# Attention queries regrouped by GpSimd copies, and end blocks padded with zeros to 128 rows, in an encoder layer on one core

## The chip, the cores and the metric

The kernel runs on one core of a Trainium2 chip. Time is device time in microseconds of one execution, and the median of several runs is the number that counts. The traces quoted here come from one further execution under the profiler.

## What is computed

One layer of a bidirectional encoder over 2048 tokens of width 1024: an input projection, eight heads of dilated attention, four heads of a gated recurrence (HGRN2), an output projection, and a mixture of 16 experts. The change touches the attention alone. Each head of width 64 runs three patterns, and in each of them the sequence falls into `dilation` interleaved subsequences, inside which a query sees the keys up to 64 places away:

```python
DILATED_PATTERNS = ((128, 1), (512, 4), (2048, 16))

def dilated_window_attention(q, k, v, window, dilation, slopes):
    half = window // (2 * dilation)          # 64 in every pattern
    ...
    band = jnp.abs(delta) <= half
    mask = band & key_ok
    bias = -slopes[:, None, None] * (dilation * jnp.abs(delta))
    s = jnp.einsum('brnqhd,brnkhd->brnhqk', qs, ks)
    s = jnp.where(mask, s + bias, NEG_INF)
    m = jnp.max(s, axis=-1, keepdims=True)
    e = jnp.exp(s - m)
    den = jnp.sum(e, axis=-1)
    num = jnp.einsum('brnhqk,brnkhd->brnqhd', e, vs)
```

The three numerators are then added with weights exp(m - max m) and divided by the denominators added in the same way.

## The kernel before

A scheduler orders the instructions of each engine ahead of time, by priorities: "mixer" work (recurrence, attention) goes first, and matmuls of the projections ("fill", into the PSUM tile `pm`) stand wherever the scheduler expected TensorE to be free. The order is fixed in the program, and each engine executes its own list in order.

The stages are: norm and input projection with the recurrence heads between its matmuls (0 to 850 us), then attention with the rest of the projection and half of the output projection as filler (850 to 1477 us), then the other half of the output projection, the routing and the experts.

In attention, `att_turn` transposes a quarter of the sequence (512 tokens, tile `x4`) into `qs` (queries) and `kh`, `kl` (keys, high and low part), with the 64 channels of a head on partitions and a second copy of them below for the low part of the queries. Both are stored in token order. `att_head` then goes through four quarters `g`. In each, `four(0, ..)` and `four(1, ..)` do four units of 128 queries for patterns 0 and 1 (dilation 1 and 4), and in the first quarter all 16 units of pattern 2 (dilation 16) are done as well. `block` takes two units (pattern 2: four):

- scores: per unit two matmuls into the PSUM tile `pS`. The stationary operand is `qs[:, q0:q0 + dil*127 + 1:dil]`, 128 queries with a step of `dil`; the moving operands are 256, 192 (at an end of a subsequence) or 128 keys of `kh` and `kl`, with the same step;
- VectorE adds the bias table and finds the extreme value (line 612), ScalarE takes exp (line 613), TensorE transposes the result in pieces (line 618), VectorE or ScalarE copies it to `eT` (lines 622 to 635), and TensorE multiplies it with the values `vp` into `pn` (line 641, two passes each). At an end of a subsequence one of the two pieces has 64 rows instead of 128.

The quarter's results go through DRAM (`num_d`), since patterns 0 and 2 hold the tokens in another arrangement: `n0` and `n2` are written by DMA, read back into `cb` beside pattern 1's result `cb[:, 2]`, combined on VectorE (lines 689 to 698), and written to `mix_d`. `cb` has three buffers that take turns over quarters.

Of the kernel before, what the change touches and what calls it, by code (L numbers as in the profile page):

```python
# [45 lines left out]
def encoder_layer(ctx, tc, x, norm1_w, w_in, q_norm_w, k_norm_w, lb_f, lb_b, o_norm_w, w_out,  # L46
# [454 lines left out]
    def att_setup(p):  # L501
        T = {}
        dl = p.tile([128, 512], F32, name="ex", bufs=4)
        T["ad"], T["mk"] = [], []
        for v, (base, w) in enumerate(((-64, 256), (0, 128))):
            a = p.tile([128, w], F32, name=f"ad{v}", bufs=1)
            pool.iota(dl[:, :w], pattern=[[1, w]], base=base, channel_multiplier=-1,
                      allow_small_or_imprecise_dtypes=True)
            dve.tensor_scalar(a, dl[:, :w], -1.0, None, op0=OP.mult)
            dve.tensor_tensor(a, a, dl[:, :w], op=OP.max)  # L510
            m = p.tile([128, w], F32, name=f"mk{v}", bufs=1)
            dve.tensor_scalar(m, a, 64.5, 1e30, op0=OP.is_gt, op1=OP.mult)
            T["ad"].append(a)
            T["mk"].append(m)
        wq = p.tile([128, 1], F32, name="wq", bufs=1)
        wk = p.tile([128, 1], F32, name="wk", bufs=1)
        for s in range(2):
            pool.dma_start(wq[s * 64:(s + 1) * 64, :], q_norm_w.rearrange("o d -> d o"))
            pool.dma_start(wk[s * 64:(s + 1) * 64, :], k_norm_w.rearrange("o d -> d o"))
        dve.tensor_scalar(wq, wq, -0.125, None, op0=OP.mult)  # L520
        T["wq"], T["wk"] = wq, wk
        for n in ("qs", "kh", "kl"):
            T[n] = p.tile([128, S], F32R, name=n, bufs=1)

        T["vp"] = [p.tile([128, n, 65], F32, name=f"vp{i}", bufs=1) for i, n in enumerate((17, 20, 16))]
        for vp in T["vp"]:
            dve.memset(vp[:, :, 64:65], 1.0)
        return T

    def att_load(p, T, h, g):  # L530

        u, s2 = h // 2, h % 2
        for j in range(2):

            x4 = p.tile([128, 4, 128], F32, name="x4", bufs=4)
            sp.dma_start(x4[:, :, :64],
                         dram_ap(qk_d, (u * S + g * 512) * 256 + 128 * j + 64 * s2,
                                 [[256, 128], [128 * 256, 4], [1, 64]]))
            pool.tensor_copy(x4[:, :, 64:], x4[:, :, :64])
            T["x4", g, j] = x4  # L540

    def att_values(T, h, g):

        voff = 64 * h
        v0, v1 = T["vp"][0], T["vp"][1].rearrange("p (r b) c -> p b r c", b=5)
        for b in (g, 4)[:1 + g // 3]:
            lo, n = (0, 64) if b == 0 else (128 * b - 64, 128 if b < 4 else 64)
            sp.dma_start(v1[:n, b, :, :64], dram_ap(v_d, voff + lo * 2048, [[2048, n], [512, 4], [1, 64]]))
        if g == 0:
            sp.dma_start(v0[:64, 0, :64], dram_ap(v_d, voff, [[512, 64], [1, 64]]))  # L550
        b0 = max(4 * g, 1)
        sp.dma_start(v0[:, b0:4 * g + 4, :64],
                     dram_ap(v_d, voff + (128 * b0 - 64) * 512, [[512, 128], [128 * 512, 4 * g + 4 - b0], [1, 64]]))
        if g == 3:
            sp.dma_start(v0[:64, 16, :64], dram_ap(v_d, voff + (S - 64) * 512, [[512, 64], [1, 64]]))

    def att_turn(T, g):

        sl = slice(g * 512, (g + 1) * 512)
        qs, kh, kl = T["qs"], T["kh"], T["kl"]  # L560
        for j in range(2):
            pt = (pa, pb)[j]()
            for i in range(4):
                pe.transpose(pt[:, i * 128:(i + 1) * 128], T["x4", g, j][:, i], ident)
            if j == 0:
                act.activation(qs[:, sl], pt, AF.Copy, scale=T["wq"])
                dve.scalar_tensor_tensor(qs[64:, sl], pt[64:], T["wq"][64:], qs[64:, sl].bitcast(F32),
                                         op0=OP.mult, op1=OP.subtract)
# [8 lines left out]
    def att_head(p, T, h):  # L577
# [2 lines left out]
        tabs = []  # L580
        for pat, (tw, v) in enumerate(((256, 0), (256, 0), (128, 1))):
            tab = p.tile([128, tw], F32, name=f"tab{pat}", bufs=2 - pat // 2)
            dve.scalar_tensor_tensor(tab, T["ad"][v], slope * 4 ** pat, T["mk"][v], op0=OP.mult, op1=OP.add)
            tabs.append(tab)

        def unit(pat, n):

            if pat == 2:
                return n, 16, n, 0, 128, [(0, 128, n)]
# [4 lines left out]
            blk = [(lo, 128 - lo, b0 + i), (128, hi - 128, b0 + i + 1)]  # L594
            return r + dil * 128 * i, dil, r + dil * (128 * i - 64 + lo), lo, hi, blk

        def block(pat, n0, units, w, nst, pnum):
# [5 lines left out]
            for j, (q0, dil, k0, lo, hi, blk) in enumerate(units):  # L603
# [5 lines left out]
            for j, (q0, dil, k0, lo, hi, blk) in enumerate(units):  # L609
# [4 lines left out]
            sizes = []  # L614
            for j, un in enumerate(units):
                for lo, nk, b in un[5]:
                    c = j * w + lo // 128 * 128
                    pe.transpose(pT[:nk, c:c + 128], ex[:, j * w + lo:j * w + lo + nk], ident)  # L618
                    sizes.append(nk)
            if min(sizes) == 128:  # L620
                if n0 % 8 < 6:
                    dve.tensor_copy(eT, pT)  # L622
                else:
                    act.activation(eT, pT, AF.Copy)
            elif sizes[:2] == sizes[2:]:
                for i in range(2):
                    ev, pv = (t[:sizes[i]].rearrange("p (j i c) -> p i j c", j=2, i=2)[:, i] for t in (eT, pT))
                    act.activation(ev, pv, AF.Copy)
            else:
                c = 0  # L630
                while c < 4:
                    e = c + 1
                    while e < 4 and sizes[e] == sizes[c]:
                        e += 1
                    act.activation(eT[:sizes[c], c * 128:e * 128], pT[:sizes[c], c * 128:e * 128], AF.Copy)
                    c = e
            for j, un in enumerate(units):
                nb = len(un[5])
                for i, (lo, nk, b) in enumerate(un[5]):
                    c = j * w + lo // 128 * 128  # L640
                    pe.matmul(pnum[:, n0 % 4 + j, :], eT[:nk, c:c + 128], vp[:nk, b, :],  # L641
                              start=i == 0, stop=i == nb - 1)

        def four(pat, n4, nst):

            per = 4 if pat == 2 else 2
            pnum = pn([128, 512])[:, :260].rearrange("p (j c) -> p j c", j=4)
            for n in range(n4, n4 + 4, per):
                block(pat, n, [unit(pat, n + i) for i in range(per)], 512 // per, nst, pnum)
            act.activation(nst[:, :, :65], pnum, AF.Copy)  # L650

        for g in range(4):
            cb = p.tile([128, 3, 4, 66], F32, name="cb", bufs=3)
            n0 = p.tile([128, 4, 66], F32, name="n0", bufs=2)
            four(0, 4 * g, n0)
            row = g * 512 * 66
            sp.dma_start(dram_ap(num_d, h * S * 66 + row, [[66, 128], [128 * 66, 4], [1, 66]]), n0)
# [175 lines left out]
    with mixer():  # L835
# [3 lines left out]
        for g in range(4):  # L839
            att_load(ap_, AT, 0, g)  # L840
            att_values(AT, 0, g)
            if g < 2:
                att_turn(AT, g)
    heads(0)
    unit_qk(2)
# [345 lines left out]
```

## Time and profile before

| | |
|---|---|
| median of 3 runs | 2837.08 us (2824.97 to 2841.68) |
| profiled execution | 2828.04 us, of which the trace spans 2825.4 us |
| attention stage in the trace | 850.3 to 1476.9 us |
| TensorE busy over the span | 2728.9 us (97%) |
| VectorE, ScalarE, GpSimd busy | 1775.3, 1453.8, 128.3 us |

The profiled execution has 2.6 us around its span. Busy time of TensorE counts overlapping matmuls, so what a matmul costs is read from the distance between the starts of neighbours, not from its duration.

### The profile page before, as it was taken

Reading aid. Unit: us, or ns where it says so; the run is one execution under the profiler, and the core shown is the slowest. Engines: PE = TensorE matmul, PEld = TensorE weight load, DVE = VectorE, ACT = ScalarE, POOL = GpSimd, SP = SyncE. Lnnn points to the kernel's source line nnn. Section 1 sums busy time; section 2 is a strip of 40 time slices with the busy share of each in tenths; the row PEclk is TensorE's granted clock in tenths of the full one; section 3 lists DMA queues with packets and bytes.
Section 4 is the critical chain, followed back from the end, with each engine's and each line's share of the span. In section 5 each row is a group of like instructions: output and inputs, shape, how many; then the busy total and the mean of one; then the engine's idle time right before and its main releaser. Section 6 shows DMA issues by size and latency. Waiting matters only on the chain.

```text
span 2825.4 us, 59470 instructions
## 1 busy us (share of the span) xinstructions
PE 2728.9 (97%) x23462; PEld 2574.3 (91%) x23462; DVE 1775.3 (63%) x4396; ACT 1453.8 (51%) x2829; POOL 128.3 (5%) x157
## 2 busy tenths in 40 slices
PE   8999999999999999999999959999999999999998
PEld 8999999899999999989898849999999999999997
DVE  6627887888865455756566565555555555555553
ACT  6636666677645444644354434444444444444442
POOL 0000000000000000000000000000000000000000
PEclk9999999999999999999999969999999999999999
DMA  9887767777767555555547526666666666666663
GB/s 301 258 248 215 235 210 226 208 228 231 222 209 201 153 133 157 152 161 157 146 131 274 175 73 212 206 206 208 209 209 209 208 208 207 207 207 206 206 196 102
DMA packets 557062, 558.73 MB, mean 198 GB/s; under 512 B 142944, under 2 KB 507488, under 8 KB 556784
## 3 DMA queue, kind: packets, MB, share of 16 engines
q1 hardware_dynamic: 547248, 521.31, 59.1%
q0 software_dynamic: 9536, 33.64, 5.3%
q8 instruction: 184, 3.01, 0.4%
q14 instruction: 94, 0.77, 0.1%
HBM read 453.92 MB, written 100.93 MB: 196 GB/s over the span
## 4 chain that ended last, share of the span: by engine, by line
PE 83%; DMA 8%; DVE 7%; ACT 2%; issue 1%; SPq 0%; POOLq 0%; POOL 0%; DVEq 0%; ACTq 0%
PE mpg L1107 9%; PE mpg L1109 9%; PE mpg L1108 9%; PE pm L236 6%; PE pm L238 6%; PE pm L237 6%; PE pn L641 5%; PE mpy L1142 4%; PE mpy L1144 4%; PE mpy L1143 4%; PE pa L607 2%; PE pa L608 2%; PE pb L618 2%; PE pm L749 2%; PE pm L750 2%; PE pm L751 2%
## 5 line engine op out<-in xcount | busy, mean ns | idle before, releaser
L1091 DVE TENSOR_TENSOR mlo<-mraw,mhi 128x1024 fp32r<-128x1024 f32 x384 | 470.3, 1225 | 461.2 <-ACT mhi L1090 460.6
L1090 ACT ACTIVATE mhi<-mraw 128x1024 fp32r<-128x1024 f32 x384 | 406.9, 1060 | 582.5 <-PE mpg L1108 402.3
L1107 PE MATMUL mpg<-xh,mhi 128*128 128x256 f32 x2048 | 579.8, 283 | 0.0
L1109 PE MATMUL mpg<-xh,mlo 128*128 128x256 f32 x2048 | 579.2, 283 | 0.0
L1108 PE MATMUL mpg<-xl,mhi 128*128 128x256 f32 x2048 | 576.6, 282 | 0.0
L1108 PEld LDWEIGHTS mpg<-xl,mhi 128*128 128x128 f32 x2048 | 387.6, 189 | 0.6
L1107 PEld LDWEIGHTS mpg<-xh,mhi 128*128 128x128 f32 x2048 | 386.7, 189 | 1.1 <-ACT xh L1063 0.4
L1109 PEld LDWEIGHTS mpg<-xh,mlo 128*128 128x128 f32 x2048 | 384.1, 188 | 0.0
L236 PE MATMUL pm<-whi,hth 128*128 128x256 f32 x1280 | 368.2, 288 | 13.5 <-ACT est L200 10.2
L237 PE MATMUL pm<-wlo,hth 128*128 128x256 f32 x1280 | 366.9, 287 | 3.8 <-DVE wlo L169 3.7
L238 PE MATMUL pm<-whi,hlo 128*128 128x256 f32 x1280 | 366.9, 287 | 0.0
L236 PEld LDWEIGHTS pm<-whi,hth 128*128 128x128 f32 x1280 | 245.6, 192 | 16.3 <-ACT est L200 12.3
L237 PEld LDWEIGHTS pm<-wlo,hth 128*128 128x128 f32 x1280 | 245.4, 192 | 6.2 <-DVE wlo L169 5.2
L238 PEld LDWEIGHTS pm<-whi,hlo 128*128 128x128 f32 x1280 | 245.4, 192 | 0.4
L236 PE MATMUL pm<-hth,whi 128*128 128x256 f32 x768 | 220.6, 288 | 2.7 <-ACT est L200 2.6
L238 PE MATMUL pm<-hth,wlo 128*128 128x256 f32 x768 | 220.1, 288 | 1.6 <-DVE wlo L169 1.6
L237 PE MATMUL pm<-hlo,whi 128*128 128x256 f32 x768 | 219.0, 285 | 0.0
L1142 PE MATMUL mpy<-mhi,hh 128*128 128x512 f32 x512 | 205.9, 403 | 0.0
L1143 PE MATMUL mpy<-mlo,hh 128*128 128x512 f32 x512 | 203.9, 398 | 0.0
L1144 PE MATMUL mpy<-mhi,hl 128*128 128x512 f32 x512 | 202.8, 396 | 0.0
L641 PEld LDWEIGHTS pn<-vp,eT 128*128 128x128 f32 (+1 forms) x1280 | 166.2, 192 | 14.8 <-issue 1.9
L641 PE MATMUL pn<-vp,eT 128*128 128x65 f32 (+1 forms) x1280 | 178.0, 276 | 1.4 <-DVE eT L622 1.2
(328 smaller groups left out, 5406.8 us busy)
## 6 DMA issues: line engine op xcount, KB each, us to landing
hlo<-lo_d SPq DMA_DIRECT2D x480, 256.0 KB, 4.0
mraw<-in_w_expert_gate_dram SPq DMA_DIRECT2D x64, 1024.0 KB, 5.4
mraw<-in_w_expert_up_dram SPq DMA_DIRECT2D x64, 1024.0 KB, 5.1
mraw<-in_w_expert_down_dram SPq DMA_DIRECT2D x64, 1024.0 KB, 5.1
wraw<-in_w_in_dram SPq DMA_DIRECT2D x128, 128.0 KB, 4.2
out_dram<-oxt SPq DMA_DIRECT2D x32, 512.0 KB, 3.7
pf_d<-est SPq DMA_DIRECT2D x96, 128.0 KB, 3.8
cb<-num_d SPq DMA_DIRECT2D x32, 264.0 KB, 3.0
```

The costliest lines, as they stand in the source:

```text
L236: pe.matmul(o, l[0], r[0], start=kc == 0, stop=False)
L237: pe.matmul(o, l[0], r[1], start=False, stop=False)
L238: pe.matmul(o, l[1], r[0], start=False, stop=kc == KC - 1)
L641: pe.matmul(pnum[:, n0 % 4 + j, :], eT[:nk, c:c + 128], vp[:nk, b, :], start=i == 0, stop=i == nb - 1)
L1090: act.activation(hi, src, AF.Copy)
L1091: dve.tensor_sub(lo, src, hi.bitcast(F32))
L1107: pe.matmul(o, hi[:, k, :], xh[:, k, :], start=k == 0, stop=False)
L1108: pe.matmul(o, hi[:, k, :], xl[:, k, :], start=False, stop=False)
L1109: pe.matmul(o, lo[:, k, :], xh[:, k, :], start=False, stop=k == KC - 1)
L1142: pe.matmul(o, hh[:, f, ts], hi[:, cs], start=f == 0, stop=False)
L1143: pe.matmul(o, hh[:, f, ts], lo[:, cs], start=False, stop=False)
L1144: pe.matmul(o, hl[:, f, ts], hi[:, cs], start=False, stop=f == KC - 1)
```

## The change

`qs` is stored grouped by the residue of the token number modulo 16, so that pattern 2's 128 queries lie side by side. For patterns 0 and 1 GpSimd copies each four's 512 queries into a new tile `qc` (two buffers) in the order of use: one copy for pattern 0, four for pattern 1. The keys stay as they were. At the ends of subsequences the scores' tile `ex` gets 64 columns of zeros from GpSimd, `vp` gets 64 rows of zeros once, and all pieces have 128 rows. The mask table is rebuilt per head on VectorE. `cb` goes from three buffers to two.

```diff
     def att_turn(T, g):
-        qs, kh, kl = T["qs"], T["kh"], T["kl"]
+        qs = T["qs"].rearrange("p (r a) -> p r a", r=16)[:, :, 32 * g:32 * g + 32]
+        kh, kl = T["kh"], T["kl"]
...
             if j == 0:
-                act.activation(qs[:, sl], pt, AF.Copy, scale=T["wq"])
+                pt = pt.rearrange("p (a r) -> p r a", r=16)
+                act.activation(qs, pt, AF.Copy, scale=T["wq"])
...
     def att_head(p, T, h):
-            dve.scalar_tensor_tensor(tab, T["ad"][v], slope * 4 ** pat, T["mk"][v], op0=OP.mult, op1=OP.add)
+            dve.tensor_scalar(tab, T["ad"][v], 64.5, 1e30, op0=OP.is_gt, op1=OP.mult)
+            dve.scalar_tensor_tensor(tab, T["ad"][v], slope * 4 ** pat, tab, op0=OP.mult, op1=OP.add)
+        def queries(pat, g):
+            qc = p.tile([128, 512], F32R, name="qc", bufs=2)
+            v = qs.rearrange("p (c r a) -> p c r a", c=4, r=4)[:, :, :, 32 * g:32 * g + 32]
+            if pat:
+                for r in range(4):
+                    pool.tensor_copy(qc[:, r * 128:r * 128 + 128].rearrange("p (a c) -> p a c", c=4),
+                                     v[:, :, r, :].rearrange("p c a -> p a c"))
+            else:
+                pool.tensor_copy(qc.rearrange("p (a c r) -> p a c r", c=4, r=4), v.rearrange("p c r a -> p a c r"))
+            return qc
...
-                qa = qs[:, q0:q0 + dil * 127 + 1:dil]
+                q = qc[:, j * 128:j * 128 + 128]
...
-                pe.matmul(pS[:, c], qa, kh[:, k0:e:dil], start=True, stop=False)
-                pe.matmul(pS[:, c], qa, kl[:, k0:e:dil], start=False, stop=True)
+                pe.matmul(pS[:, c], q, kh[:, k0:e:dil], start=True, stop=False)
+                pe.matmul(pS[:, c], q, kl[:, k0:e:dil], start=False, stop=True)
+                if lo:
+                    pool.memset(ex[:, j * w:j * w + lo], 0.0)
+                if hi < w:
+                    pool.memset(ex[:, j * w + hi:j * w + w], 0.0)
...
-            if min(sizes) == 128:
-                if n0 % 8 < 6:
-                    dve.tensor_copy(eT, pT)
-                else:
-                    act.activation(eT, pT, AF.Copy)
-            elif sizes[:2] == sizes[2:]:
...
+            if n0 % 8 < 6:
+                dve.tensor_copy(eT, pT)
+            else:
+                act.activation(eT, pT, AF.Copy)
...
         for g in range(4):
-            cb = p.tile([128, 3, 4, 66], F32, name="cb", bufs=3)
+            cb = p.tile([128, 3, 4, 66], F32, name="cb", bufs=2)
```

GpSimd's doubling of `x4` (64 columns copied beside themselves) moves from `att_load` to a function of its own, `att_twice`, which is called two quarters later.

The scheduler makes a new order of all this. On TensorE, the last filler ahead of the end of attention stood at the beginning of the last head before, after all but 88 of the 768 score matmuls, of which a head has 96 (`pm` is the filler's bank, `woh` and `wol` the output weights, `pn` takes the value products, `x` a quarter to transpose):

```order
L750 MATMUL pm<-wol,mh 128x512
L751 MATMUL pm<-woh,ml 128x512
L641 MATMUL pn<-vp_12941,eT 128x65 x4
L564 MATMUL pa<-ident,x_19891 128x128 x4
L641 MATMUL pn<-vp_12941,eT 128x65 x4
L618 MATMUL pb<-ident,ex 64x128
L618 MATMUL pb<-ident,ex 128x128 x3
L607 MATMUL pa<-kh,qs 128x192
L608 MATMUL pa<-kl,qs 128x192
```

In the changed program the last filler stands here, and 208 score matmuls come behind it:

```order
L764 MATMUL pm<-woh,ml 128x512
L762 MATMUL pm<-woh,mh 128x512
L649 MATMUL pn<-vp_12936,eT 128x65 x4
L763 MATMUL pm<-wol,mh 128x512
L764 MATMUL pm<-woh,ml 128x512
L628 MATMUL pa<-kh,qc 128x256
L629 MATMUL pa<-kl,qc 128x256
L628 MATMUL pa<-kh,qc 128x256
L629 MATMUL pa<-kl,qc 128x256
L640 MATMUL pb<-ident,ex 128x128 x4
```

The same filler is used up earlier: score matmuls of 2.2 heads stand behind it instead of 0.9.

On VectorE, in the last head, pattern 1's scores of the third quarter (into `cb_20472`) stood ahead of the first quarter's combination (`cb_20101`), and waited for matmuls and an exp (the names in brackets are semaphores of what the row waits for):

```order
L612 ISA cb_20472 128x1
L612 ISA ex_20521,cb_20472<-pa_20520,tab1_20097 128x256
L612 ISA cb_20472 128x1
L689 TENSOR_REDUCE cm_20351<-cb_20101 128x4 [waits DMAHW3_49]
L690 TENSOR_TENSOR cw_20350<-cm_20351,cb_20101 128x12 [waits DVE_49]
L622 COPY eT_20478<-pb_20477 128x512 [waits PE_49]
L612 ISA ex_20542,cb_20472<-pa_20541,tab1_20097 128x256 [waits PE_49,Activation_49]
L612 ISA cb_20472 128x1
```

In the changed program the third quarter's `cb_20742` is the buffer of the first quarter's `cb_20351`. Its first row stands behind the combinations of the first two quarters and waits for a DMA, the write of `cb_20351` to `mix_d`:

```order
L711 TENSOR_TENSOR cb_20351<-cb_20351 128x4x64 [waits DVE_49]
L705 TENSOR_TENSOR cdd_20730<-cw_20727,cb_20628 128x12 [waits Activation_49]
L706 TENSOR_REDUCE cd_20729<-cdd_20730 128x4 [waits DVE_49]
L707 RECIPROCAL cd_20729<-cd_20729 128x4 [waits DVE_49]
L708 TENSOR_TENSOR cw_20727<-cw_20727,cd_20729 128x12 [waits DVE_49]
L709 TENSOR_TENSOR cb_20628<-cb_20628,cw_20727 128x12x64 [waits DVE_49]
L711 TENSOR_TENSOR cb_20628<-cb_20628 128x4x64 [waits DVE_49]
L637 ISA ex_20798,cb_20742<-pa_20797,tab1_20345 128x256 [waits DMAHW6_49]
L637 ISA cb_20742 128x1
L637 ISA ex_20798,cb_20742<-pa_20797,tab1_20345 128x256
```

So the scores of the third quarter moved behind the way of the first quarter's result through DRAM; the same holds in every head.

On GpSimd, in the last head, copies of queries, zeros and doublings of `x` form one list, where before there was only a doubling of `x` now and then:

```order
L605 COPY qc<-qs 128x512
L633 MEMSET ex 128x64 x2
L631 MEMSET ex 128x64
L546 COPY x_20263<-x_20263 128x4x64
L602 COPY qc<-qs 128x128 x4
L546 COPY x_20265<-x_20265 128x4x64
L605 COPY qc<-qs 128x512
L631 MEMSET ex 128x64 x4
L602 COPY qc<-qs 128x128 x4
```

The two buffers of `qc` take turns, so a copy waits for the score matmuls of the four before the last.

## Rows read from the trace of the kernel before

**Rows 1.** Windows: stretch, length, busy of PE, PEld, DVE, ACT, POOL; clock, DMA share, GB/s.

```profile
850.30:1476.90 626.60, 623.96 (x4328) 591.66 (x4328) 372.02 (x1335) 309.33 (x786) 26.45 (x60) 0.98 0.56 154
1425.20:1476.90 51.70, 50.58 (x343) 48.28 (x342) 32.87 (x139) 28.99 (x78) 0.00 (x0) 0.90 0.37 100
1440.00:1455.00 15.00, 15.00 (x87) 15.00 (x87) 8.59 (x48) 8.16 (x24) 0.00 (x0) 0.66 0.01 2
```

**Rows 2.** Windows of the filler bank pm alone: the same columns without POOL.

```profile
1425.40:1476.90 51.50, 0.21 (x1) 0.00 (x0) 0.69 (x1) 0.00 (x0) 0.90 0.37 101
```

**Rows 3.** Groups by form, 850 to 1485 us: busy us, mean ns, idle before.

```profile
L607 PE MATMUL pa<-kh,qs 128*128 128x128 f32 x128 | 50.4, 405 | 0.0
L607 PE MATMUL pa<-kh,qs 128*128 128x192 f32 x80 | 34.3, 429 | 0.4 <-DVE qs L567 0.3
L641 PE MATMUL pn<-vp,eT 64*128 64x65 f32 x160 | 34.3, 296 | 0.1
```

**Rows 4.** Timeline of PE, pattern 0, then a filler matmul: start us, duration us.

```profile
988.06 0.28 PE L608 MATMUL pa<-kl,qs 128*128 128x256 f32 x1
988.17 0.28 PE L237 MATMUL pm<-wlo,hth 128*128 128x256 f32 x1
```

**Rows 5.** Timeline of PE, pattern 2.

```profile
877.82 0.39 PE L607 MATMUL pa<-kh,qs 128*128 128x128 f32 x1
878.04 0.39 PE L608 MATMUL pa<-kl,qs 128*128 128x128 f32 x1
```

**Rows 6.** Timeline of PE, pattern 1, then a filler matmul.

```profile
901.45 0.42 PE L608 MATMUL pa<-kl,qs 128*128 128x256 f32 x1
901.68 0.30 PE L236 MATMUL pm<-whi,hth 128*128 128x256 f32 x1
```

**Rows 7.** Timeline of weight loads at the same place.

```profile
901.47 0.21 PEld L236 LDWEIGHTS pm<-whi,hth 128*128 128x128 f32 x1
```

**Rows 8.** Timeline of PE, pattern 1 at an end of a subsequence.

```profile
1431.97 0.42 PE L607 MATMUL pa<-kh,qs 128*128 128x192 f32 x1
1432.20 0.42 PE L608 MATMUL pa<-kl,qs 128*128 128x192 f32 x1
```

**Rows 9.** Timeline of PE, value products, 64-row operands among them.

```profile
870.03 1.53 PE L641 MATMUL pn<-vp,eT 64*128 64x65 f32 x8
871.39 0.39 PE L564 MATMUL pb<-ident,x 128*128 128x128 f32 x2
```

**Rows 10.** Timeline of PE, value products with 128 rows alone.

```profile
984.62 1.90 PE L641 MATMUL pn<-vp,eT 128*128 128x65 f32 x16
986.35 0.39 PE L618 MATMUL pb<-ident,ex 128*128 128x128 f32 x2
```

**Rows 11.** Groups by form, 850 to 1485 us, VectorE.

```profile
L622 DVE COPY eT<-pb 128x512 f32<-128x512 f32 x96 | 65.8, 688 | 59.1 <-PE pb L618 58.3
L567 DVE SCALAR_TENSOR_TENSOR qs<-pa,wq,qs 64x512 fp32r<-64x512 f32 x31 | 23.5, 757 | 14.2 <-ACT qs L566 13.5
```

**Rows 12.** DMA issues of the page's kind: count, size, median us to landing.

```profile
mix_d<-cb SPq DMA_DIRECT2D x32, 128.0 KB, 3.3
```

**Rows 13.** Timeline of SP, last head: issues.

```profile
1457.59 0.32 SPq L676 DMA_DIRECT2D num_d<-n  x1
...
1471.24 0.56 SPq L699 DMA_DIRECT2D mix_d<-cb  x1
```

**Rows 14.** Timeline of SP, first head: issues.

```profile
900.69 0.42 SPq L676 DMA_DIRECT2D num_d<-n  x1
...
921.45 0.58 SPq L699 DMA_DIRECT2D mix_d<-cb  x1
```

**Rows 15.** Groups by form, whole span, GpSimd.

```profile
L539 POOL COPY x<-x 128x256 f32<-128x256 f32 x64 | 28.1, 438 | 560.1 <-DMA x<-qk_d 516.8 <-PE pn L641 23.1 <-PE pm L238 20.2
L796 POOL TENSOR_SCALAR h<-oxt,osy 128x1024 f32<-128x1024 f32 x1 | 2.9, 2852 | 124.0 <-DVE osy L114 124.0
```

More of the change, by code (lines that the diff above doesn't have):

```diff
@@ L503, in att_setup @@
         dl = p.tile([128, 512], F32, name="ex", bufs=4)
-        T["ad"], T["mk"] = [], []
+        T["ad"] = []
         for v, (base, w) in enumerate(((-64, 256), (0, 128))):
@@ L510, in att_setup @@
             dve.tensor_tensor(a, a, dl[:, :w], op=OP.max)
-            m = p.tile([128, w], F32, name=f"mk{v}", bufs=1)
-            dve.tensor_scalar(m, a, 64.5, 1e30, op0=OP.is_gt, op1=OP.mult)
             T["ad"].append(a)
-            T["mk"].append(m)
         wq = p.tile([128, 1], F32, name="wq", bufs=1)
@@ L527, in att_setup @@
             dve.memset(vp[:, :, 64:65], 1.0)
+        for vp, n, step in ((T["vp"][0], 17, 17), (T["vp"][1], 20, 5)):
+            for b in range(0, n, step):
+                dve.memset(vp[:64, b, :64], 0.0)
+                dve.memset(vp[64:, b + step - 1, :64], 0.0)
         return T
@@ L538, in att_load, with att_twice @@
                                  [[256, 128], [128 * 256, 4], [1, 64]]))
+            T["x4", g, j] = x4
+    def att_twice(T, g):
+        for j in range(2):
+            x4 = T["x4", g, j]
             pool.tensor_copy(x4[:, :, 64:], x4[:, :, :64])
-            T["x4", g, j] = x4
     def att_values(T, h, g):
@@ L546, in att_values @@
         for b in (g, 4)[:1 + g // 3]:
-            lo, n = (0, 64) if b == 0 else (128 * b - 64, 128 if b < 4 else 64)
-            sp.dma_start(v1[:n, b, :, :64], dram_ap(v_d, voff + lo * 2048, [[2048, n], [512, 4], [1, 64]]))
+            lo, r = (0, slice(64, 128)) if b == 0 else (128 * b - 64, slice(0, 128 if b < 4 else 64))
+            sp.dma_start(v1[r, b, :, :64], dram_ap(v_d, voff + lo * 2048, [[2048, r.stop - r.start], [512, 4], [1, 64]]))
         if g == 0:
-            sp.dma_start(v0[:64, 0, :64], dram_ap(v_d, voff, [[512, 64], [1, 64]]))
+            sp.dma_start(v0[64:, 0, :64], dram_ap(v_d, voff, [[512, 64], [1, 64]]))
         b0 = max(4 * g, 1)
@@ L565, in att_turn @@
             if j == 0:
-                act.activation(qs[:, sl], pt, AF.Copy, scale=T["wq"])
-                dve.scalar_tensor_tensor(qs[64:, sl], pt[64:], T["wq"][64:], qs[64:, sl].bitcast(F32),
+                pt = pt.rearrange("p (a r) -> p r a", r=16)
+                act.activation(qs, pt, AF.Copy, scale=T["wq"])
+                dve.scalar_tensor_tensor(qs[64:], pt[64:], T["wq"][64:], qs[64:].bitcast(F32),
                                          op0=OP.mult, op1=OP.subtract)
@@ L593, in unit, with block @@
             lo, hi = (64 if i == 0 else 0), (192 if i == nb - 1 else 256)
-            blk = [(lo, 128 - lo, b0 + i), (128, hi - 128, b0 + i + 1)]
-            return r + dil * 128 * i, dil, r + dil * (128 * i - 64 + lo), lo, hi, blk
-        def block(pat, n0, units, w, nst, pnum):
+            return r + dil * (128 * i - 64 + lo), dil, lo, hi, [b0 + i, b0 + i + 1]
+        def block(pat, n0, qc, units, w, nst, pnum):
             tab, vp = tabs[pat], vps[pat]
@@ L602, in block @@
             eT = p.tile([128, 512], F32, name="eT", bufs=2)
-            for j, (q0, dil, k0, lo, hi, blk) in enumerate(units):
-                qa = qs[:, q0:q0 + dil * 127 + 1:dil]
+            for j, (k0, dil, lo, hi, blk) in enumerate(units):
+                q = qc[:, j * 128:j * 128 + 128]
                 c = slice(j * w + lo, j * w + hi)
                 e = k0 + dil * (hi - lo - 1) + 1
-                pe.matmul(pS[:, c], qa, kh[:, k0:e:dil], start=True, stop=False)
-                pe.matmul(pS[:, c], qa, kl[:, k0:e:dil], start=False, stop=True)
-            for j, (q0, dil, k0, lo, hi, blk) in enumerate(units):
+                pe.matmul(pS[:, c], q, kh[:, k0:e:dil], start=True, stop=False)
[4 more added lines that the diff above has]
+                    pool.memset(ex[:, j * w + hi:j * w + w], 0.0)
+            for j, (k0, dil, lo, hi, blk) in enumerate(units):
                 c = slice(j * w + lo, j * w + hi)
@@ L613, in block @@
                 act.activation(ex[:, c], ex[:, c], AF.Exp, bias=m, scale=-1.0)
-            sizes = []
-            for j, un in enumerate(units):
[L616 to L619, printed above, removed]
-            if min(sizes) == 128:
-                if n0 % 8 < 6:
-                    dve.tensor_copy(eT, pT)
-                else:
-                    act.activation(eT, pT, AF.Copy)
-            elif sizes[:2] == sizes[2:]:
[L626 to L642, printed above, removed]
+            for c in range(0, 512, 128):
+                pe.transpose(pT[:, c:c + 128], ex[:, c:c + 128], ident)
+            if n0 % 8 < 6:
+                dve.tensor_copy(eT, pT)
+            else:
+                act.activation(eT, pT, AF.Copy)
+            for j, un in enumerate(units):
+                nb = len(un[4])
+                for i, b in enumerate(un[4]):
+                    c = j * w + i * 128
+                    pe.matmul(pnum[:, n0 % 4 + j, :], eT[:, c:c + 128], vp[:, b, :], start=i == 0, stop=i == nb - 1)
         def four(pat, n4, nst):
@@ L647, in four @@
             pnum = pn([128, 512])[:, :260].rearrange("p (j c) -> p j c", j=4)
+            qc = qs[:, n4 * 128:n4 * 128 + 512] if pat == 2 else queries(pat, n4 // 4)
             for n in range(n4, n4 + 4, per):
-                block(pat, n, [unit(pat, n + i) for i in range(per)], 512 // per, nst, pnum)
+                block(pat, n, qc[:, n % 4 * 128:], [unit(pat, n + i) for i in range(per)], 512 // per, nst, pnum)
             act.activation(nst[:, :, :65], pnum, AF.Copy)
         for g in range(4):
-            cb = p.tile([128, 3, 4, 66], F32, name="cb", bufs=3)
+            cb = p.tile([128, 3, 4, 66], F32, name="cb", bufs=2)
             n0 = p.tile([128, 4, 66], F32, name="n0", bufs=2)
+            if g == 0:
+                att_twice(T, 2)
+                att_twice(T, 3)
+            elif g > 1 and h < 7:
+                att_twice(T, g - 2)
             four(0, 4 * g, n0)
@@ L842, in encoder_layer @@
             if g < 2:
+                att_twice(AT, g)
                 att_turn(AT, g)
```

2 lines of the change are left out of this document (1 added, 1 removed).

## Prediction

> **What bounds the kernel now.** I read the windows by stage first. In the attention stage TensorE shows 623.96 us busy of 626.60, VectorE 372.02 and ScalarE 309.33 [rows 1], so its own list of instructions sets the pace, and a matmul costs the distance between two starts. The filler's windows then show where this holds by filler alone: over the last 51.5 us of the stage the filler's bank has one matmul [rows 2], and there VectorE is busy for 32.87 us and the granted clock is 0.90, with 0.66 in the middle, a mix of the levels 1.2 and 2.4 GHz; TensorE is busy without a gap in that window, which holds the last head's pattern 2, so its strided queries and the lower clock go together [rows 1]. Last I read the timeline of TensorE for the price of each kind of matmul.
>
> **What the strided queries cost.** A score matmul of pattern 0 over 256 keys takes 0.11 to 0.12 us to the next start [rows 4], one of pattern 2 over 128 keys 0.22 (0.217 over a run of them) [rows 5], one of pattern 1 over 256 keys 0.23 [rows 6], and over 192 keys also 0.23 [rows 8]. Counts: line 607 has 128 matmuls of pattern 2 and 80 of 192 keys [rows 3], 16 of these in pattern 0; line 608 has as many; by the code pattern 1 thus has 128 matmuls of 192 keys and 128 of 256.
>
> What contiguous queries give back depends on the moving keys, which stay strided. The filler matmul behind the 256-key one starts 0.23 us later [rows 6], though its weights began to load at 901.47, 0.02 us after that matmul's start [rows 7], and a filler with its weights on the way otherwise follows in 0.12 us [rows 4]. I take it that the 256 strided keys themselves need 0.23, or 0.92 ns each, against 0.46 contiguous. Then 256 keys gain nothing, 192 keys fall from 0.236 to 0.177 (128 x 0.059 = 7.6 us), and 128 keys from 0.217 to 0.118 (256 x 0.099 = 25.3 us). No row shows keys with a step of 16 alone; the bounds are 0.109, the contiguous price, and 0.217, no gain. I take the step-4 price, since it comes from the same operand.
>
> The Trainium skill (Advanced Engine Details and Errata, SBUF Cachelines) says that reads want at least two hits on each 16-byte line and pay a penalty when every access goes to another one. This speaks against half of the change: queries of either step are cured, keys of either step are not. By it alone pattern 1 keeps part of its price and pattern 2's keys are no worse than pattern 1's, as in the sum; without it the sum is that of the first rival. The trace agrees for step 4 (0.23 against 0.12); no row here shows step 16 by itself.
>
> **End blocks.** Eight products with two 64-row units take 1.36 us [rows 9], sixteen with 128 rows 1.73, so eight 0.87 [rows 10]. 160 products have 64 rows [rows 3]: 32 blocks of pattern 1 with four, 16 of pattern 0 with two. At 0.49 and half of it: 15.7 + 4.0 = 19.7 us.
>
> Sum on TensorE: 7.6 + 25.3 + 19.7 = 52.6 us, 6.6 per head.
>
> **What it adds.** VectorE gets 32 more copies of 0.688 us [rows 11], 22 us, which ScalarE loses in smaller pieces, and 24 table operations over at most half a copy's columns, under 0.7 each. Query writes now read PSUM with a step: between today's 0.757 us [rows 11] and twice that (as the strided load), 32 times on each engine. All of this lies beside TensorE, with VectorE at 59% of the stage; without cover in the last heads it is 1.5 us per quarter. GpSimd's copies: 256 elements take 0.438 us, 1024 in another operation 2.852 [rows 15], so 512 take 0.88 to 1.43, and up to about 2 if the four copies of pattern 1 each have a fixed part. A four without filler takes TensorE some 5 us (a head is 20 blocks, and the bare 51.7 us hold 88 of its 96 score matmuls: 2.6 us or more a block, two blocks a four), and `qc` has two buffers, so a copy has one whole four to hide behind; zeros and doublings stand between them. I cost GpSimd at nothing; a copy that came late would cost its excess in up to 64 fours.
>
> **The buffer that goes.** With two `cb` buffers the third quarter's pattern-1 scores wait on VectorE until the first quarter's result has reached `mix_d`. Behind that row stand all further scores and copies, for which ScalarE and the transposes wait. The way begins with pattern 2's last product: write `n2`, read `cb`, combine, write `mix_d`. In the last head it took 13.65 us from issue to issue [rows 13] plus 3.3 to land [rows 12], 17.0; in the first head, among other DMAs, 20.76 [rows 14] + 3.3 = 24.1. What TensorE has to do meanwhile I counted in the new order, from that product to the first transpose that needs those scores, at the prices above: 21.6 to 28.8 us in heads 0 to 5 (mean 23.6, with 9 to 18 us of filler), but 11.6 and 10.8 in heads 6 and 7, which have none. So two bubbles of 6 us, 12 together, and some 3 us over the other six. Filler that stands in those six bubbles is missing at the end: that is why 2.2 heads now run without it.
>
> In these 2.2 heads TensorE's gain counts only as far as VectorE and ScalarE, which each block passes through, keep up: 208 of 768 score matmuls, 14.2 us of the gain; I take half as lost, 7. The clock, 0.66 for 15 us today, may stay up where pattern 2 is denser, and fall in the bubbles; I charge 3 us. Losses: 12 + 3 + 7 + 3 = 25.
>
> **Sum.** 52.6 - 25 = 27.6 us off the profiled 2828.0: 2800.4, a ratio of 0.990. That execution lies 0.3% below the median of the runs shown, so on the median's footing 2809.
>
> **Rivals.** (Times on the median's footing; 0.5%, about 14 us, is what a measurement can tell from no change.)
>
> First, strided keys are not a limit, and the 0.23 behind pattern 1 comes from the strided load alone. For it: 192 and 256 keys show the same 0.23 [rows 6, 8]. Against it: the filler's early load. Pattern 1 then gains 256 x 0.118 = 30.2 and pattern 2 256 x 0.108 = 27.6, 77.5 with the ends; less 25 and the tail's half of the extra (3.4), 49 us: 2788.
>
> Second, the bare end eats the gain: all 14.2 us of it lost there, the bubbles' 15, and 30 us more at half clock, of which half is lost, 15. 52.6 - 44 = 8 us: 2829, no change that can be told. For it: 0.66 at full occupation [rows 1]; against it: VectorE had 19 us free in those 51.7.
>
> Third, slower, by the `cb` wait in every head. If the way through DRAM takes c us in all heads, the loss is 6 x (c - 23.6) + 2 x (c - 11.2) beside 10 for tail and clock. It meets 52.6 at c = 25.8; at 28 it is 26 + 34 + 10 = 70, 17 us slower: 2855. For it: 24.1 in the first head, where SP's queue was full of filler loads [rows 14]; against it: 17.0 in the last, and there the combination shared VectorE with scores that now wait behind it.
>
> **Chances.** Forecast 0.50; strided keys free 0.14; eaten at the end 0.20; slower by the wait 0.16. The first two are faster by over 0.5%, the third within, the fourth slower: 0.64, 0.20, 0.16. The range reaches from some way beyond the first rival, if the losses are also smaller (2778), to over the second and toward the third (2842).
>
> **What would show it.** Weight loads at the scores fall from 0.31 to 0.19 us everywhere; 64-row products are gone, and four in a block take 0.87 us. Pattern 1 over 256 keys still at 0.23, over 192 at 0.18, pattern 2 at 0.12: right for the forecast; 0.12 for all: first rival; pattern 2 at 0.2: 25 us less. VectorE's wait for `mix_d<-cb` appears at the first row of the third quarter, near 6 us in the last two heads and near none in the others; if it is long in heads 0 to 5, the third rival. The last filler should stand some 110 us ahead of the stage's end, with TensorE idle for about 20 us in that part and a lower clock. TensorE waiting for GpSimd at the scores would make the forecast wrong, since that is costed at nothing.

## The result, and the profile after

The changed kernel takes 2802.3 us in the median (2799.1 to 2819.8, four runs) where the kernel before takes 2838.9, now with a fourth run: a ratio of 0.989, with a 95% interval of 0.986 to 0.992. This ratio and those below are taken over the fast runs, which all of them are, and differ a little from the quotient of the two medians, here 0.987. The profiled execution after took 2802.6 us against 2828.0 before, 25.4 us less. The windows by stage show where (stretch, length, busy time of PE, PEld, DVE, ACT and POOL, clock, DMA share, GB/s):

```profile
850.30:1452.00 601.70, 578.01 (x4301) 550.64 (x4301) 403.28 (x1385) 287.12 (x705) 121.11 (x293) 0.96 0.58 160
1452.00:2800.80 1348.80, 1300.26 (x9376) 1199.81 (x9374) 781.83 (x1480) 608.53 (x938) 92.08 (x74) 0.98 0.62 196
...
1321.60:1452.00 130.40, 111.49 (x778) 107.00 (x777) 94.13 (x350) 66.22 (x166) 28.73 (x74) 0.84 0.38 96
1325.00:1345.00 20.00, 18.62 (x103) 18.16 (x102) 14.24 (x47) 9.38 (x22) 4.94 (x13) 0.57 0.61 164
```

The attention stage, counted to the first transposes of the output projection behind it (tile `mx`), is 601.7 us long instead of 626.6 [rows 1]: the whole gain. TensorE had 2.6 us without work in it before and has 23.7 now, so it is busy for 46 us less, and 21 us of that turned into pauses. The last 130.4 us have no filler (51.5 before [rows 2]), and there the clock is 0.84, with 0.57 in one stretch of 20 us.

The timeline of TensorE gives the new distances (start, duration): pattern 2 over 128 keys, pattern 1 over 256 and over 192, and eight value products with the matmul behind them.

```profile
961.66 0.35 PE L628 MATMUL pa<-kh,qs 128*128 128x128 f32 x1
961.82 0.31 PE L629 MATMUL pa<-kl,qs 128*128 128x128 f32 x1
961.94 0.31 PE L628 MATMUL pa<-kh,qs 128*128 128x128 f32 x1
962.05 0.31 PE L629 MATMUL pa<-kl,qs 128*128 128x128 f32 x1
...
1137.85 0.47 PE L628 MATMUL pa<-kh,qc 128*128 128x256 f32 x1
1138.12 0.43 PE L629 MATMUL pa<-kl,qc 128*128 128x256 f32 x1
1138.35 0.43 PE L628 MATMUL pa<-kh,qc 128*128 128x256 f32 x1
1138.59 0.43 PE L629 MATMUL pa<-kl,qc 128*128 128x256 f32 x1
...
1166.00 0.36 PE L629 MATMUL pa<-kl,qc 128*128 128x192 f32 x1
1166.18 0.36 PE L628 MATMUL pa<-kh,qc 128*128 128x192 f32 x1
1166.35 0.36 PE L629 MATMUL pa<-kl,qc 128*128 128x192 f32 x1
...
858.14 1.00 PE L649 MATMUL pn<-vp,eT 128*128 128x65 f32 x8
858.95 0.36 PE L236 MATMUL pm<-whi,hth 128*128 128x256 f32 x1
```

Pattern 2 stands at 0.11 to 0.12 us (the first, behind a transpose, at 0.16), where it had 0.217 [rows 5]. Pattern 1 over 256 keys still needs 0.23 to 0.24 [rows 6]; over 192 keys it needs 0.17 to 0.18 instead of 0.236 [rows 8]. Eight value products at the end of a subsequence take 0.81 to 0.84 us instead of 1.36 [rows 9]. One distance fell that the neighbours do not show, that of the first score matmul in a block of pattern 1. It is 0.27 us here (1137.85 to 1138.12; 0.28 at the median), and was 0.40 in the kernel before:

```profile
900.10 0.58 PE L607 MATMUL pa<-kh,qs 128*128 128x256 f32 x1
900.50 0.42 PE L608 MATMUL pa<-kl,qs 128*128 128x256 f32 x1
```

The weight loads of these scores, by line (minimum, median, maximum in ns), have a median of 0.19 us, where it was 0.31; the first row is from the kernel before:

```profile
L607 PEld LDWEIGHTS pa<-kh,qs x384: 187/309/345, 850.7 to 1471.6; 128*128 128x128 f32 x192
...
L628 PEld LDWEIGHTS pa<-kh,qc x256: 186/190/337, 851.0 to 1450.2; 128*128 128x128 f32 x128
L628 PEld LDWEIGHTS pa<-kh,qs x128: 186/192/337, 874.0 to 1418.0; 128*128 128x128 f32 x128
```

What GpSimd got, by groups (busy us, mean ns, idle before):

```profile
L602 POOL CAST qc<-qs 128x128 fp32r<-128x128 f32 x128 | 53.8, 464 | 89.7 <-PE pa L629 89.6
L605 POOL CAST qc<-qs 128x512 fp32r<-128x512 f32 x32 | 35.8, 1117 | 137.0 <-PE pa L629 53.9 <-issue 46.0 <-DVE n L637 32.3
```

A copy of pattern 0 takes 1.12 us, the four of pattern 1 take 1.86 at the mean. TensorE's waits in the stage (total, times, longest) name no GpSimd; the first is new:

```profile
PE pa L628 <- DVE cb L637: 12.0, 3, 6.2
PE pn L649 <- DVE eT L642: 3.5, 4, 1.5
...
PE pb L640 <- ACT ex L638: 1.5, 3, 1.1
```

The three are 2.6 us in head 5, 6.2 in head 6 and 3.2 in the last head. The one in head 6 reads like this on SP's queue, then VectorE, then TensorE:

```profile
1369.90 1.22 SPq L689 DMA_DIRECT2D num_d<-n  x1
...
1383.07 0.57 SPq L712 DMA_DIRECT2D mix_d<-cb  x1
```

```profile
1378.42 0.17 DVE L702 TENSOR_REDUCE cm<-cb 128x4 f32<-128x12 f32 x1 [0.58 <-DMA cb<-num_d]
...
1382.62 0.43 DVE L711 TENSOR_TENSOR cb<-cb 128x256 f32<-128x256 f32 x1
...
1384.37 0.89 DVE L711 TENSOR_TENSOR cb<-cb 128x256 f32<-128x256 f32 x2
1385.40 0.42 DVE L637 CUSTOM_DVE_ANT_0 ex<-pa,tab 128x256 f32<-128x256 f32 x1
```

```profile
1379.14 1.02 PE L649 MATMUL pn<-vp,eT 128*128 128x65 f32 x8
1386.33 0.55 PE L628 MATMUL pa<-kh,qc 128*128 128x256 f32 x1 [6.16 <-DVE cb L637]
```

The first quarter's sum is ready at 1383.05, its way to `mix_d` is issued at 1383.07, and the third quarter's first scores run at 1385.40, 2.3 us later. VectorE shows no idle time there, since the second quarter's combination lies in the wait; TensorE has nothing to do for 6 us. Whether the buffer or the combination holds the scores up cannot be told from these rows; the next kernel has a third buffer, and no such pause.

### The profile page after: what moved, and what is told of

It is laid out like the page before. It is cut to its first block, busy times and chain, and to the rows that moved or that the text cites. A ratio compares the mean times of both kernels' runs of the same rounds, so it can differ in the third digit from the quotient of the medians.

```text
span 2800.8 us, 59888 instructions
## 1 busy us (share of the span) xinstructions
PE 2680.9 (96%) x23462; PEld 2531.2 (90%) x23462; DVE 1808.3 (65%) x4460; ACT 1433.1 (51%) x2749; POOL 226.8 (8%) x397
## 4 chain that ended last, share of the span: by engine, by line
PE 80%; DVE 8%; DMA 7%; ACT 2%; issue 1%; SPq 0%; POOLq 0%; POOL 0%; DVEq 0%; ACTq 0%
PE mpg L1121 9%; PE mpg L1123 9%; PE mpg L1122 9%; PE pm L236 5%; PE pm L237 5%; PE pm L238 5%; PE pn L649 4%; PE mpy L1156 4%; PE mpy L1158 4%; PE mpy L1157 4%; PE pb L640 2%; PE pm L762 2%; PE pm L764 2%; PE pm L763 2%; DMA gz<-pf_d 2%; PE pa L629 2%
## 5 line engine op out<-in xcount | busy, mean ns | idle before, releaser
L649 PEld LDWEIGHTS pn<-vp,eT 128*128 128x128 f32 x1280 | 163.8, 199 | 6.2 <-DVE eT L642 4.6
L649 PE MATMUL pn<-vp,eT 128*128 128x65 f32 x1280 | 165.2, 277 | 3.5 <-DVE eT L642 3.5
```

The costliest lines, as they stand in the source:

```text
L649: pe.matmul(pnum[:, n0 % 4 + j, :], eT[:, c:c + 128], vp[:, b, :], start=i == 0, stop=i == nb - 1)
```

## The experiments

The theory with which I went in: TensorE's list is 54 us shorter at full clock (256 x 0.104 = 26.6 of pattern 2, 128 x 0.060 = 7.7 of the 192-key matmuls, 20 of the end blocks), and it comes back by the pauses of the two-buffer `cb` in the last heads and the half-clock stretches beside them. Its rivals were that the stretches without filler are bound by VectorE and ScalarE anyway, and that GpSimd's copies cost something.

| kernel | ratio to before | 95% interval |
|---|---|---|
| the change | 0.9889 | 0.9861 to 0.9917 |
| before, two `cb` buffers | 1.0102 | 1.0067 to 1.0137 |
| before, end blocks alone | 0.9950 | 0.9935 to 0.9966 |
| before, dense queries without copies | 0.9885 | 0.9850 to 0.9919 |
| change, three `cb` buffers | 0.9821 | 0.9792 to 0.9850 |
| change, third buffer in heads 6, 7 | 0.9862 | 0.9831 to 0.9892 |
| change, third buffer in heads 0 to 5 | 0.9823 | 0.9793 to 0.9853 |
| change, copies twice | 0.9893 | 0.9861 to 0.9924 |
| three buffers, eT shared evenly | 0.9791 | 0.9767 to 0.9816 |
| three buffers, pattern 1 keys dense | 0.9776 | 0.9741 to 0.9810 |

**Three buffers again.** The room comes from the second buffers of `tab0` and `tab1`, which was not tried by itself.

```diff
-            tab = p.tile([128, tw], F32, name=f"tab{pat}", bufs=2 - pat // 2)
+            tab = p.tile([128, tw], F32, name=f"tab{pat}", bufs=1)
...
-            cb = p.tile([128, 3, 4, 66], F32, name="cb", bufs=2)
+            cb = p.tile([128, 3, 4, 66], F32, name="cb", bufs=3)
```

> The changed kernel with three cb buffers again (tab0 and tab1 get one buffer each, which makes the room). In the changed kernel TensorE stands still for 12.0 us behind line 637's cb, 6.2 in head 6 and 3.5 in head 7, and half-clock stretches follow. Theory A (the two cb buffers cost these pauses): they go, and with them part of the half-clock time, so 12 to 20 us come off against the changed kernel; ratio to the kernel before 0.982 to 0.985. Rival B (without filler the last 2.2 heads are bound by VectorE and ScalarE, whatever the buffers): the last filler still stands 125 to 130 us ahead of the stage's end, the pauses only move, less than 5 us come off; ratio 0.987 to 0.990.

Measured: 0.9821, some 19 us better by the two ratios (14 by the two medians). The windows of the stage and of its part without filler, and TensorE's waits for the same lines:

```profile
850.30:1444.80 594.50, 577.74 (x4428) 551.01 (x4427) 406.42 (x1403) 293.62 (x717) 125.67 (x302) 0.99 0.61 166
1391.60:1444.80 53.20, 46.92 (x369) 44.57 (x368) 39.96 (x156) 30.41 (x77) 9.02 (x25) 0.97 0.38 110
```

```profile
PE pn L649 <- DVE eT L642: 7.6, 7, 1.9
...
PE pa L628 <- DVE cb L637: 0.9, 1, 0.9
```

The wait for `cb` has gone from 12.0 to 0.9 us and the stage's clock from 0.96 to 0.99. TensorE's idle time in the stage fell less, from 23.7 to 16.8 us, since its waits for `eT` rose from 3.5 to 7.6. And the stretch without filler is 53 us again and not 130, which theory A did not say: the buffers also decide where the filler goes.

**Two buffers alone, in the kernel before.**

```diff
-            cb = p.tile([128, 3, 4, 66], F32, name="cb", bufs=3)
+            cb = p.tile([128, 3, 4, 66], F32, name="cb", bufs=2)
```

> The kernel before with two cb buffers and nothing else. Theory A: VectorE's scores of the third quarter wait for mix_d in the last head, which has no filler there; a pause of about 6 us on TensorE in the last head, 0 to 3 in head 6, and next to none in heads 0 to 5; 5 to 9 us slower, ratio 1.002 to 1.003. Rival B: the slower old matmuls cover the way, no pause over 1 us, ratio 1.000. Third theory (the wait in every head): 6 us in each head, ratio about 1.015.

Measured: 1.0102, 29 us slower, which lies between the theories. The windows of the stage and its part without filler, and the wait over the whole stage:

```profile
850.30:1505.90 655.60, 640.48 (x4300) 606.04 (x4299) 375.89 (x1337) 307.61 (x782) 27.46 (x59) 0.93 0.53 147
1365.40:1505.90 140.50, 126.81 (x779) 121.10 (x778) 87.41 (x341) 71.85 (x187) 4.90 (x10) 0.79 0.35 88
...
1380.00:1396.00 16.00, 16.00 (x84) 14.37 (x84) 10.30 (x34) 9.53 (x26) 1.67 (x3) 0.68 0.49 111
```

```profile
PE pa L607 <- DVE cb L612: 13.0, 3, 6.0
```

The pauses are of theory A's kind, but longer and more: 2.7 us in head 5, 6.0 in head 6 and 4.3 in the last. TensorE stands idle for 12.5 us more than in the kernel before [rows 1], and with the same instructions it is busy for 16.5 us more (640.48 against 623.96). That part goes with the clock: 0.93 in the stage instead of 0.98, and 0.79 in a stretch without filler that has grown to 140 us. Read in windows of 5 us, 86 us of the stage lie at 1.2 GHz, against 31; half of the difference, 28 us, would be an upper estimate of the loss. The third row of windows shows the low clock in a stretch where TensorE has no pause at all.

**The third buffer in some heads only.** Both give the third quarter a tile of its own and let the other three share two buffers, the one in heads 6 and 7, the other in heads 0 to 5 (`h < 6`); elsewhere there are two buffers. `tab0` and `tab1` have one buffer in both.

```diff
-            cb = p.tile([128, 3, 4, 66], F32, name="cb", bufs=3)
+            cbx = g == 2 and h > 5
+            cb = p.tile([128, 3, 4, 66], F32, name="cx" if cbx else "cb", bufs=1 if cbx else 2)
```

> The changed kernel with a third cb tile for the third quarter of heads 6 and 7 alone (tab0 and tab1 with one buffer each, as where all heads had three). Theory A (the wait costs in the last two heads, where no filler stands behind it): nearly all of the gain of three buffers, ratio to the kernel before 0.982 to 0.985, no pause behind line 637's cb. Rival (in heads 0 to 5 the wait is paid in filler, which is then missing at the end): the last filler still stands about 130 us ahead of the stage's end and the half-clock stretches there stay, ratio 0.985 to 0.988.

> The changed kernel with a third cb tile for the third quarter of heads 0 to 5 alone. Theory A: the pauses of 6.2 and 3.5 us in heads 6 and 7 stay, next to nothing is won, ratio 0.987 to 0.989. Rival (heads 0 to 5 pay in filler): the last filler moves to about 50 us ahead of the stage's end, so head 6 has filler for its wait, and only the pause of the last head stays; ratio 0.983 to 0.986.

Measured: 0.9862 in heads 6 and 7, not to be told from the change; 0.9823 in heads 0 to 5, as good as three buffers everywhere. Stage and stretch without filler, first with the buffer in heads 6 and 7:

```profile
850.30:1452.20 601.90, 582.35 (x4350) 553.98 (x4348) 399.63 (x1393) 290.24 (x709) 122.28 (x297) 0.96 0.59 161
1334.50:1452.20 117.70, 104.11 (x748) 99.52 (x746) 86.86 (x333) 63.15 (x158) 26.61 (x67) 0.87 0.39 99
```

and in heads 0 to 5:

```profile
850.30:1448.20 597.90, 579.50 (x4368) 553.27 (x4367) 403.79 (x1392) 290.03 (x710) 129.18 (x301) 0.97 0.60 164
1385.40:1448.20 62.80, 55.18 (x359) 53.46 (x359) 44.84 (x167) 31.54 (x79) 12.18 (x29) 0.78 0.36 99
```

With the buffer only in the last heads no score of TensorE waits for `cb` any more, but 118 us have no filler, and TensorE still stands idle for 19.6 us of the stage (23.7 after the change). One pause has only moved: in head 6 the fourth quarter's scores now stand on VectorE behind the combinations, and TensorE waits 4.4 us for them and their exponentials. On VectorE, then TensorE:

```profile
1395.62 0.35 DVE L637 CUSTOM_DVE_ANT_0 ex<-pa,tab 128x192 f32<-128x192 f32 x1
...
1396.58 0.69 PE L640 MATMUL pb<-ident,ex 128*128 128x128 f32 x2 [4.41 <-ACT ex L638]
```

So this kernel does not show what the last heads would give without any pause. With the buffer in heads 0 to 5 the filler lasts to 63 us ahead of the end, and the pause of the last head is still there, 3.3 us. Theory A falls as to the place: the two buffers are paid for mainly in heads 0 to 5, in filler, which is then missing at the end. The tables cannot be the cause of the gain: they have one buffer in both kernels, and only the second can be told from the change.

**End blocks alone**, in the kernel before: its queries and three buffers, and of the change the zeros, the 128-row pieces and the mask table rebuilt per head.

```diff
+                if lo:
+                    pool.memset(ex[:, j * w:j * w + lo], 0.0)
...
+            for c in range(0, 512, 128):
+                pe.transpose(pT[:, c:c + 128], ex[:, c:c + 128], ident)
```

> The kernel before with the end blocks alone: zeros in ex and vp, all transposes and value products on 128 rows, queries strided as before, three cb buffers. Theory A: TensorE loses 0.5 us in each of 32 blocks and 0.23 in each of 16, 20 us, of which 0 to 6 are lost again as filler ends earlier; ratio 0.993 to 0.995. Rival B: the 64-row products were hidden behind VectorE and ScalarE in the blocks, so 5 us at most, ratio 0.998 to 1.000.

Measured: 0.9950, 14 us (10 to 18). Theory A holds: 20 us by TensorE's distances, and about 6 lost again (its idle time in the stage is some 10 us longer than in the kernel before).

**Dense queries alone**, in the kernel before.

```diff
-                qa = qs[:, q0:q0 + dil * 127 + 1:dil]
+                qa = qs[:, (n0 + j) * 128:(n0 + j) * 128 + 128]
```

> The kernel before with contiguous stationary queries and no copies: each score matmul reads 128 neighbouring columns of qs, so the queries of patterns 1 and 2 are the wrong ones; no GpSimd work, old end blocks, three cb buffers. Theory A (GpSimd's copies cost nothing): pattern 2 falls from 0.217 to 0.113 us, pattern 1 over 192 keys from 0.236 to 0.176 and over 256 stays at 0.233; 34 us off TensorE's list, 3 to 8 lost again at the end of the stage, ratio 0.989 to 0.991. Rival (the copies cost the changed kernel something that its waits don't name): without them 45 us or more come off, ratio below 0.985.

Measured: 0.9885, 33 us (23 to 43), with medians of 0.113, 0.176 and 0.233 us for the three kinds of matmul. With the end blocks that is 47 us, and three buffers with the whole change gave 51: the parts add up, and no price of the copies shows, within the some 10 us that the intervals leave.

**Copies twice.**

```diff
-                for r in range(4):
+                for r in (0, 1, 2, 3, 0, 1, 2, 3):
...
+                for _ in range(2):
+                    pool.tensor_copy(qc.rearrange(...), v.rearrange(...))
```

> The changed kernel with each of GpSimd's query copies made twice into the same tile. Theory A (the copies of 1.1 us for pattern 0 and 1.5 to 2.2 for pattern 1 lie behind a whole four): still no wait of TensorE for qc, ratio to the kernel before 0.987 to 0.991, as with single copies. Rival (the cover is nearly used up in the stretches without filler): TensorE waits for qc in most fours there, 10 us or more slower than with single copies, ratio 0.993 or more.

Measured: 0.9893 against 0.9889. GpSimd makes twice the copies and TensorE waits once for one of them:

```profile
PE pa L629 <- DVE cb L638: 16.6, 4, 7.8
...
PE pb L641 <- POOL qc L602: 2.9, 1, 2.9
```

So the copies had at least their own length as cover nearly everywhere. That twice the copies cost nothing is not shown: the wait for `cb` is 16.6 us here and 12.0 with single copies, and TensorE's idle time in the stage is 30.5 us against 23.7, a difference that the interval of the ratio could hide.

**The step of the keys.** Two kernels with pattern 1's keys at a step of 2 and of 8, pattern 2's contiguous in both.

```diff
+                dil = (1, 2, 1)[pat]
+                k0 = min(k0, S - 512)
```

```diff
+                dil = (1, 8, 1)[pat]
+                k0 = k0 % 4 if pat == 1 else k0
```

> The changed kernel with pattern 1's keys taken at a step of 2 and pattern 2's contiguous, so both patterns score the wrong keys; all counts and widths stay. Theory A (a strided moving key costs 0.92 ns once each read has a 16-byte line of its own, as at step 4): at step 2 two reads share a line, and 256 keys fall from 0.233 to about 0.12 us, 192 from 0.176 to 0.11; pattern 2 stays at 0.11. The rule of lines is that of the Trainium skill (Advanced Engine Details and Errata, SBUF Cachelines). Rival: any step costs the same, 0.23 and 0.176 stay; or the price goes by the step, 0.16 to 0.18 for 256 keys.

> The changed kernel with pattern 1's keys at a step of 8 from the start of the row and pattern 2's contiguous, so both patterns score the wrong keys. Theory A (the price of a strided key does not grow beyond step 4): 256 keys stay at 0.23 us, 192 at 0.18. Rival (the price grows with the step, and pattern 2's 0.113 at step 16 is hidden behind its weight loads): 0.3 us or more for 256 keys.

Measured on the timeline of TensorE, first 256 keys at step 2:

```profile
1126.34 0.42 PE L630 MATMUL pa<-kh,qc 128*128 128x256 f32 x1
1126.57 0.42 PE L631 MATMUL pa<-kl,qc 128*128 128x256 f32 x1
1126.80 0.42 PE L630 MATMUL pa<-kh,qc 128*128 128x256 f32 x1
```

and at step 8:

```profile
1189.43 0.40 PE L630 MATMUL pa<-kh,qc 128*128 128x256 f32 x1
1189.65 0.40 PE L631 MATMUL pa<-kl,qc 128*128 128x256 f32 x1
```

256 keys take 0.23 us at step 2 (median 0.229; 192 keys 0.173) and 0.22 at step 8 (0.219; 0.165). Both steps are at the price of step 4, so the first rival of the step-2 kernel holds: any step costs the same. Pattern 2's contiguous 128 keys stand at 0.112, against 0.113 with step 16, so at that width the keys' step can't be seen. These two were run once each, and their times are not compared.

**Pattern 1's keys contiguous**, with three buffers.

```diff
+                dil = (1, 1, 16)[pat]
+                k0 = min(k0, S - 256)
```

> Three cb buffers, and pattern 1's keys contiguous, so that pattern 1 scores the wrong keys. Theory A (the step of the moving keys is what is left of the price): 256 keys fall from 0.233 to 0.12 us, 192 from 0.176 to 0.11, 23 us off TensorE's list, 3 to 8 of them lost again where no filler stands; ratio 0.974 to 0.977. Rival (0.23 comes from something else in pattern 1, such as the writes of qc or the banks): no change of these distances, ratio 0.982.

Measured: 256 keys at 0.120 us, 192 at 0.112, so the step is the whole of what was left. But the ratio is 0.9776, 13 us for 23, and the interval reaches into that of three buffers alone. Half of it was lost again in waits; the largest of them has risen from 7.6 us:

```profile
PE pn L651 <- DVE eT L644: 13.7, 13, 2.6
```

**The copies of `eT` shared evenly**, with three buffers.

```diff
-            if n0 % 8 < 6:
+            if n0 % 8 < 4:
                 dve.tensor_copy(eT, pT)
             else:
                 act.activation(eT, pT, AF.Copy)
```

> Three cb buffers, and the copies of eT shared evenly: those of pattern 0 and 1 two and two, those of pattern 2 in turn, where VectorE had three of four and all of pattern 2 in every second four. Theory A (what is left in the stretches without filler is TensorE waiting for VectorE's eT, 7.6 us with three buffers): 3 to 6 us come off against three buffers alone, ratio 0.979 to 0.981. Rival (the exponentials on ScalarE then come late): no gain or a loss up to 6 us, ratio 0.982 to 0.985.

Measured: 0.9791, the fastest complete kernel here. TensorE's wait for VectorE's `eT` falls from 7.6 us:

```profile
PE pn L649 <- DVE eT L642: 2.8, 3, 1.5
```

This agrees with theory A, but the interval overlaps that of three buffers alone. Against the change and against the kernel before it is clear.

## Why the prediction was right, and where it was not

The forecast of 2809 us stands beside 2802 measured, and on the footing of the two profiles 2800.4 beside 2802.6. The prices of the matmuls were right between neighbours: pattern 2 fell to 0.113 us (forecast 0.118), 192 keys to 0.176 (0.177), 256 keys stayed; 34.3 us at full clock where the sum had 32.9. The sum has nothing for the first matmul of a block of pattern 1 over 256 keys, which fell from 0.40 to 0.28 us: in 32 blocks some 4 us, an estimate from the two distances shown. **The first rival** falls with these prices: strided keys are a limit, and only contiguous ones brought 0.12. The Trainium skill (Advanced Engine Details and Errata, SBUF Cachelines) asks for at least two hits on a 16-byte line, which fp32 keys at a step of 2 have, so that step should be free by it; here step 2 cost 0.229 us for 256 keys and step 4 0.233, and the measurement decides. The sum didn't hang on it. The assumption that step 16 has the step-4 price stays untested, since 128 keys show no difference even from contiguous ones.

**End blocks.** Forecast 0.49 us per block with four such products and 19.7 in all; measured 0.52, and by itself 14 us of the whole time.

**What it adds.** VectorE's busy time in the stage rose by 31 us (372.02 in [rows 1], 403.28 now), nine more than the copies alone, and the time fell all the same; the query writes with a step in PSUM kept their 0.757 us, the lower bound. GpSimd at nothing was right as far as the times can tell, some 9 us, by the kernel without copies and by the one with two of each.

**The buffer, the tail and the clock** are the terms that were off, while the losses came out near the 25 us of the text: 54 less the 25 of the two profiles is 29. Of these, 21 are idle time of TensorE (23.7 us against 2.6), and the other 8, an estimate, are matmuls that took longer than at full clock (54 less the 46 by which it is less busy).

The pauses behind `cb`, 12.0 us in heads 5, 6 and 7, are the forecast's "two bubbles of 6 us" and the 3 us over the other heads. The one in the last head is shorter than forecast: there the way took 12.96 us up to the first score on VectorE (1430.25 to 1443.21), not 17.0. TensorE's other waits grew by 9 us, where the text charged the tail with 7. The clock cost some 8 where it had 3: read in windows of 5 us, the stage before has 31 us at 1.2 GHz, the changed one 51 and the one with three buffers 17. The text charged the pauses 3 us too much and the tail and the clock 7 too little; that the sum came so close is partly luck.

What the text had too small is thus the price of the buffer by way of the filler. It had seen that filler standing in the waits of the early heads "is missing at the end", and charged that end and its clock with 10 us together, where 17 came. A third buffer in heads 0 to 5, which brings the filler back, gave the whole difference; one in the last two heads, where the bubbles were forecast, gave none that can be told.

**The second rival** named this mechanism and had too much of it: 30 us more at half clock, where 20 came. **The third**, the slower case, was right that two buffers cost more than their bubbles: alone they cost 1.0%. It did not come true because the wait did not come as a pause in every head, but as filler used up early.

What stays open: why the clock falls where it does. After the change most of its low stretches begin in or just behind a pause of TensorE (the one at 1326 behind 2.6 us of standing still). But in the kernel before, the one at 1440 lay in strided pattern 2 without a pause [rows 1], and with two buffers alone it fell in the stretch without filler while TensorE was busy throughout. So a pause isn't needed for it, and no run here shows what is. Nor was one buffer for the tables tried without a third tile for `cb`.

## What to carry to other kernels

A buffer given up to make room can be paid far from where the wait stands: where filler covers the wait, look at how far ahead of the stage's end the filler now runs out, and find the room in a tile whose users are all on one engine, as the tables are here. Price the stationary and the moving operand apart, each by a row in which only one of them is strided. When TensorE's list gets shorter, look at the copy between transpose and product in the stretches without filler: here it became TensorE's longest wait, and moving part of it to the other engine is the next thing to try, though its gain is not yet clear of the noise.

## What the runs showed of the hardware

A moving fp32 operand with a step of 2, 4 or 8 costs about 0.9 ns a column: 0.229 us for 256 keys at step 2, 0.233 at step 4, 0.219 at step 8, against 0.120 contiguous. So there is no gain from a small step and no further loss up to 8. A stationary operand with a step costs more to load, 0.31 us in the median against 0.19, and the 0.217 us between two 128-key matmuls became 0.113 when it was made contiguous and nothing else was changed. And a large part of a missing buffer's price came with TensorE's clock and not as a pause: with two buffers the kernel before was 29 us slower, with 12.5 us more idle time on TensorE in the stage (15.1 against 2.6), 16.5 us more busy time for the same instructions, and a clock of 0.93 instead of 0.98.
